# Gate projections moved among the convolution's taps, other PSUM banks for a values projection, and two products moved to the front of the Strassen stage

## The chip, the cores and the metric

The kernel runs on one core of one Trainium2 chip. The metric is the device time of one execution in microseconds. A core has five engines with an instruction queue each: TensorE (PE, matmuls; PEld are its weight loads), VectorE (DVE), ScalarE (ACT), GpSimd (POOL) and SyncE (SP, which here only issues transfers). An engine works through its queue in order and waits on semaphores of the others.

## What is computed

One layer of a trunk with four token mixers side by side, for 512 tokens of width 2048, in float32. With `h = rms_norm(x)`, one wide projection `h @ w_in` is cut into the inputs of the branches and four merge gates:

```python
A  differential attention (8 heads, two softmax maps per head, ...)
B  sliding-window (128) grouped-query attention (16 q heads / 4 kv heads) ...
C  Mamba-2 SSD (16 heads, 2 B/C groups, state 128, conv 4, chunk 128) ...
D  Conformer convolution module (GLU -> causal depthwise conv 31 -> LayerNorm
   -> swish), causal
Each branch (width 1024) is multiplied by a SiLU gate path, projected to D_MODEL,
merged as sum_i sigmoid(g_i(h)) * branch_i, then one output projection and a
residual add.
```

The change touches the SiLU gates of branches A and D, the values of branch A, the convolution of branch D, and the four merge gates, whose projections are computed by a Strassen scheme.

## The kernel before, in words

`h` is held transposed in SBUF, split into a high part `hh` and a low part `hl` (each element is their sum). Every weight piece of 512 KB is loaded by SyncE into `wr`; ScalarE casts it to `wh` (L274) and VectorE makes the rest `wl` (L275). Each product is three matmuls: `hh·wh`, `hl·wh`, `hh·wl` (L388 to L390, with `proj`; 48 matmuls of 128x512 for 128 columns of the projection). `next_piece` prepares pieces up to six ahead in the order of the list `seq`. A scheduler that keeps the data dependencies decides, from costs that it assumes, in which order each engine gets its instructions; the kernel's text only gives the first wish.

The stages on TensorE, with their times in the profiled execution:

- to 328 us: norm, scan of branch C. Its end lies beside `values(0)`, the values projection for the first four heads (L617 to L619). A block of the scan loads `se` (POOL, L555), scales, exponentiates and multiplies it (L559 to L570), and its two kinds of matmul (L576, L579) add into the bank `o`, which VectorE then reads (L583). `values(0)` adds four blocks of 128 tokens in four PSUM banks: three `acc` banks and the `o` bank.
- 328 to 502 us: for each of eight channels of 128, two projections of branch D, `DV` and `DGT`. VectorE evicts them (L641, L644, with ScalarE's sigmoid and GpSimd's product L643 between) and runs 31 taps over the padded row `pad` (L646, L648) into `y`, called `keep_yl` in the trace. GpSimd adds the channels up in `csum` (L653).
- 502 to 576 us: `values(4)` for the other four heads, on the same kind of banks; the normalization over channels that needs `csum` begins beside it (`pm`).
- 576 to 665 us: eight projections `DG`, each with `silu_of` (L402 to L404: product by VectorE, sigmoid by ScalarE, product by VectorE), and the output of branch D.
- 665 to 1021 us: eight heads of differential attention, each with the projections `AQ`, `AK`, `AG` (`AG` with `silu_of`) and four blocks: scores, a biased maximum (L781), exp (L785), normalization (L786 to L789), transposes (L792), product with the values (L796).
- 1021 to 1261 us: windowed heads, in the same manner (L741 and L742 scores, L851 to L865 softmax, L869 transposes, L876 product with the values).
- 1261 to 1906 us: merge gates, eight blocks `gi` of 336 matmuls. For the first block the sums and differences of quarters of `h` are made by `make_sums` (L902 to L913: `e` pairs, written as high and low parts `s1`, `s2`, `s4` and in place of the second quarter of `hh`, `hl`), two of 16 row groups per call. A step `s1` of the list brings weights for one of eight `k`, with sums of weights made on VectorE (L235 to L237); a step `s2` those for the three products added afterwards.
- to the end: up-projections of the branches, merge, output projection.

The four accumulators of a gate block are `ba` (two `acc` banks), `bc` (`s` banks), `bd` (`tr` banks) and `bb` (`acc`, `o`). The pool `mge` behind `ev_pair()` gives `e` tiles, three buffers in turn.

Of the kernel before, what the change touches and what calls it, by code (L numbers as in the profile page):

```python
# [11 lines left out]
F32 = mybir.dt.float32  # L12
# [31 lines left out]
def build_sequence():  # L44
    seq = []

    def proj(col):
        for half in range(2):
            seq.append(("p", col, half))

    def values(h):
        for k2 in range(KT // 2):
            seq.append(("v", AV + h * P, k2 * 2, 2, S))

    for half in range(2):
        for col in (CB, CC):
            seq.append(("p", col, half))
    for g in range(2):
        if g > 0:
            proj(CB + g * P)  # L60
            proj(CC + g * P)
        for j in range(4):
            proj(CX + (g * 4 + j) * P)
        for j in range(4):
            proj(CZ + (g * 4 + j) * P)
    values(0)
    for c in range(NB):
        proj(DV + c * P)
        proj(DGT + c * P)
    values(4)  # L70
    for c in range(NB):
        proj(DG + c * P)
    for h in range(8):
        proj(AQ + h * P)
        proj(AK + h * P)
        proj(AG + h * P)
    for j in range(2):
        proj(BK + j * P)
        proj(BV + j * P)
    for j in range(8):  # L80
        proj(BQ + j * P)
        proj(BG + j * P)
    for gi in range(NGATE):
        for k in range(KH):
            seq.append(("s1", gi, k))
        for r in range(3):
            for kp in range(KH // 2):
                seq.append(("s2", gi, r, kp))
# [14 lines left out]
def hybrid_trunk(ctx, tc, x, norm_w, w_in, diff_lambda, diff_subln_w, swa_sinks, ssd_conv_w,  # L103
# [50 lines left out]
    def keep(tag):  # L154
        return yp.tile([P, S], F32, tag=tag, name="keep_" + tag)
# [62 lines left out]
        return hi, lo  # L218

    def strassen_piece(key):  # L220
        gi = key[1]
        n1, n2 = columns(gi)
        sh = [P, 2, S]
        if key[0] == "s1":
# [25 lines left out]
    def make_piece(i):  # L250
        key = seq[i]
        late = False
        if key[0] in ("s1", "s2"):
            pieces[i] = strassen_piece(key)
            return
        if key[0] == "p":
# [346 lines left out]
            G.dma_start(y_d[2, g * 4 + j], y)  # L603


    banks4 = [acc_tile, acc_tile, acc_tile, o_tile]
    vtoks = []

    def values(h):
# [12 lines left out]
        for t in range(NT):  # L622
            for e in range(4):
# [9 lines left out]
    cv = []  # L633
    csum = ph.tile([P, S], F32, tag="csum", name="csum")
    for c in range(NB):
# [10 lines left out]
        V.tensor_scalar(y, pad[:, 0:S], cols[:, NV + c:NV + c + 1], col("fb", c), op0=ALU.mult, op1=ALU.add)  # L646
        for j in range(1, 31):
            V.scalar_tensor_tensor(y, pad[:, j:j + S], cols[:, NV + j * 8 + c:NV + j * 8 + c + 1], y,  # L648
                                   op0=ALU.mult, op1=ALU.add)
        if c == 0:  # L650
            G.tensor_copy(csum, y)
        else:
            G.tensor_tensor(csum, csum, y, op=ALU.add)  # L653
        cv.append(y)
    pm = s_tile(0)
    T.matmul(pm, lhsT=ones, rhs=csum, start=True, stop=True)
    mean = tmp()
# [14 lines left out]
    rd = row_of_tokens(rs)  # L672
    rbs = ph.tile([P, S], F32, tag="rbs", name="rbs")
    A.copy(rbs, rd)
    values(4)
# [86 lines left out]
    for h in range(8):  # L762
# [169 lines left out]
    def ev_pair():  # L932
        return mge.tile([P, 2, S], F32, tag="e", name="e")

    def strassen(gi, finish, extra=None):
        ba = [acc_tile(), acc_tile()]
        bc = [s_tile(0), s_tile(1)]
        bd = [tr_tile(), tr_tile()]
        bb = [acc_tile(), o_tile()]
        for k in range(KH):  # L940
            if extra is not None and k % 2 == 0:
                extra(k // 2)
            (xh, xl), (yh, yl) = next_piece(("s1", gi, k))
            ends = (k == 0, k == KH - 1)
            for bank, st, w in ((ba, lambda t: block(k, t, 0), (xh[:, 0], xl[:, 0])),
                                (bc, lambda t: stat(2, k, t), (yh[:, 0], yl[:, 0])),
                                (bd, lambda t: block(k, t, 1), (yh[:, 1], yl[:, 1])),
                                (bb, lambda t: stat(1, k, t), (xh[:, 1], xl[:, 1]))):
                for t in range(2):
                    mm3(bank[t], st(t), w, *ends)  # L950
        u2, u3 = ev_pair(), ev_pair()
        for t in range(2):
            A.copy(u2[:, t], ba[t])
# [6 lines left out]
        for r, bank in ((0, ba), (1, bd), (2, bb)):  # L960
            for kp in range(KH // 2):
                wh, wl = next_piece(("s2", gi, r, kp))
                for j in range(2):
# [11 lines left out]
                finish(r % 2, t, r // 2, bank[t] if r == 0 else u[:, t], u[:, t])  # L975

    for gi in range(NGATE):
        def finish(half, t, right, src, dst):
            tt = half * 2 + t
            n = gi % 2 * S + right * 2 * S  # L980
            A.activation(dst, src, AF.Sigmoid, scale=rst[:, tt:tt + 1])  # L981
            G.dma_start(gate_d[gi // 2, tt][:, n:n + S], dst)  # L982

        strassen(gi, finish, make_sums if gi == 0 else None)
    close_pool("mge", "mgt", "mgw", "sab", "hp")


# [181 lines left out]
```

## Time and profile before

| | before |
|---|---|
| median of 3 runs | 2449.65 us (2446.09 to 2450.25) |
| profiled execution | 2448.79 us |
| its span, first to last instruction | 2446.4 us |
| TensorE busy | 2382.8 us, 97% |
| VectorE busy | 1557.2 us, 64% |
| ScalarE busy | 944.9 us, 39% |
| GpSimd busy | 299.8 us, 12% |

The profiled execution's own time is its span and 2.4 us around it. A busy TensorE may run at either level of its clock; the profile gives the granted clock as a share of full speed.

### The profile page before, as it was taken

The page shows a single profiled execution, that of the slowest core. Times are in us where ns is not written, and L with a number is a line of the kernel's source. Part 1 is how long each engine was busy: PE and PEld are TensorE (multiplying, and loading weights), DVE is VectorE, ACT ScalarE, POOL GpSimd, SP SyncE. Part 2 cuts the span into 40 slices and gives each one's busy share as a digit, 9 for nine tenths or more (in the row PEclk, how much of TensorE's full clock was granted, in tenths as well). Part 3 has the DMA queues.
Part 4 walks back from the last instruction along what each step waited for, and adds up shares of the span by engine and source line. Part 5 has one row for each costly group of instructions (what it writes and reads, how often), then busy time and mean ns, then how long its engine had stood idle before and what let it go on. Part 6 is the DMA issues. An engine that isn't in the chain of part 4 may idle for free.

```text
span 2446.4 us, 29178 instructions
## 1 busy us (share of the span) xinstructions
PE 2382.8 (97%) x11189; PEld 1959.1 (80%) x11189; DVE 1557.2 (64%) x2496; ACT 944.9 (39%) x1439; POOL 299.8 (12%) x312
## 2 busy tenths in 40 slices
PE   8999899989999999999978999999999999999998
PEld 7877688868888888887756888888888888888888
DVE  6586449999756565465669777787777543444323
ACT  5343122212545455455544444444444322222222
POOL 0022011210311111100000000000000002322101
PEclk9999999999999999999989999999999999999999
DMA  6343243324433333333323555455556744443423
GB/s 178 86 122 104 69 112 95 95 61 112 127 106 91 92 99 87 104 91 95 95 74 112 166 166 166 150 171 163 171 167 194 258 169 146 151 146 111 156 96 112
DMA packets 292586, 309.80 MB, mean 127 GB/s; under 512 B 13198, under 2 KB 197899, under 8 KB 292446
## 3 DMA queue, kind: packets, MB, share of 16 engines
q1 hardware_dynamic: 278174, 266.71, 36.5%
q0 software_dynamic: 10784, 34.92, 4.3%
q10 hardware_dynamic: 3488, 6.30, 0.8%
q8 instruction: 87, 1.43, 0.2%
q14 instruction: 53, 0.43, 0.1%
HBM read 278.44 MB, written 29.45 MB: 126 GB/s over the span
## 4 chain that ended last, share of the span: by engine, by line
PE 87%; DVE 10%; issue 1%; DMA 1%; ACT 1%; POOL 0%; POOLq 0%; DVEq 0%; ACTq 0%
PE acc L390 10%; PE acc L388 10%; PE acc L389 10%; DVE keep_yl L648 5%; PE acc L930 3%; PE acc L929 3%; PE acc L928 3%; PE tr L929 2%; PE tr L930 2%; PE tr L928 2%; PE s L928 2%; PE s L930 2%; PE s L929 2%; PE acc L968 2%; PE acc L969 2%; PE acc L967 2%
## 5 line engine op out<-in xcount | busy, mean ns | idle before, releaser
L274 ACT CAST wh<-wr 128x1024 fp32r<-128x1024 f32 x284 | 297.6, 1050 | 782.2 <-PE acc L389 295.3
L275 DVE TENSOR_TENSOR wl<-wr,wh 128x1024 fp32r<-128x1024 f32 x284 | 363.1, 1282 | 344.6 <-ACT wh L274 341.7
L388 PE MATMUL acc<-hh,wh 128*128 128x512 f32 x1376 | 544.7, 396 | 0.1
L390 PE MATMUL acc<-hh,wl 128*128 128x512 f32 x1376 | 541.3, 394 | 0.2 <-DVE wl L275 0.2
L389 PE MATMUL acc<-hl,wh 128*128 128x512 f32 x1376 | 540.7, 393 | 0.0
L390 PEld LDWEIGHTS acc<-hh,wl 128*128 128x128 f32 x1376 | 258.8, 188 | 53.6 <-issue 1.3
L389 PEld LDWEIGHTS acc<-hl,wh 128*128 128x128 f32 x1376 | 259.1, 188 | 53.0 <-issue 1.7
L388 PEld LDWEIGHTS acc<-hh,wh 128*128 128x128 f32 x1376 | 258.8, 188 | 52.8 <-issue 2.1
L211 ACT CAST wh<-wr 128x1024 fp32r<-128x1024 f32 x128 | 133.8, 1052 | 140.6 <-PE o L930 60.0
L648 DVE SCALAR_TENSOR_TENSOR keep_yl<-pad,cols,keep_yl 128x512 f32<-128x512 f32 x240 | 176.1, 786 | 0.7
L212 DVE TENSOR_TENSOR wl<-wr,wh 128x1024 fp32r<-128x1024 f32 x128 | 155.5, 1220 | 30.7 <-ACT wh L211 30.7
L982 POOL DMA_DIRECT2D gate_d<-e x64 | 34.5, 540 | 614.0 <-ACT e L981 598.5
L1043 POOL TENSOR_TENSOR m<-m,u 128x512 f32<-128x512 f32 x48 | 73.6, 1568 | 273.4 <-DVE u L1042 273.4
L215 ACT CAST wh<-t 128x512 fp32r<-128x512 f32 x64 | 39.7, 621 | 108.7 <-PE tr L930 69.5
L929 PE MATMUL acc<-wl,yh 128*128 128x512 f32 x192 | 74.8, 390 | 0.0
L930 PE MATMUL acc<-wh,yl 128*128 128x512 f32 x192 | 74.8, 390 | 0.0
L928 PE MATMUL acc<-wh,yh 128*128 128x512 f32 x192 | 74.1, 389 | 0.0
L247 DVE TENSOR_TENSOR t<-wr,t 128x1024 f32<-128x1024 f32 x32 | 39.1, 1223 | 46.1 <-DMA wr<-in_w_in_dram 46.1
L212 DVE TENSOR_TENSOR wl<-t,wh 128x1024 fp32r<-128x1024 f32 x32 | 39.2, 1225 | 36.4 <-ACT wh L211 36.4
L402 DVE TENSOR_TENSOR keep_yl<-acc,rb 128x512 f32<-128x512 f32 x24 | 16.6, 691 | 68.0 <-PE acc L390 68.0
L235 DVE TENSOR_TENSOR vr<-vr,wr 128x512 f32<-128x512 f32 x64 | 43.8, 688 | 25.0 <-DMA wr<-in_w_in_dram 24.9
L785 ACT ACTIVATE pr<-pr,mx 128x128 f32<-128x128 f32 (+3 forms) x64 | 35.5, 556 | 58.4 <-DVE mx L783 58.3
(461 smaller groups left out, 4960.8 us busy)
## 6 DMA issues: line engine op xcount, KB each, us to landing
wr<-in_w_in_dram SPq DMA_DIRECT2D x320, 512.0 KB, 3.8
wr<-in_w_branch_dram SPq DMA_DIRECT2D x64, 512.0 KB, 3.6
vr<-in_w_in_dram SPq DMA_DIRECT2D x32, 512.0 KB, 4.5
gate_d<-e POOLq DMA_DIRECT2D x64, 256.0 KB, 3.3
gt<-gate_d SPq DMA_DIRECT2D x16, 1024.0 KB, 5.0
wr<-in_w_out_dram SPq DMA_DIRECT2D x32, 512.0 KB, 3.5
yraw<-y_d SPq DMA_DIRECT2D x8, 1024.0 KB, 7.8
y_d<-t POOLq DMA_DIRECT2D x24, 256.0 KB, 2.6
```

Of the source, the lines that this page charges most:

```text
L211: A.copy(hi, srcs[0])
L212: V.tensor_tensor(lo, srcs[0], hi.bitcast(F32), op=ALU.subtract)
L274: A.copy(hi, raw)
L275: V.tensor_tensor(lo, raw, hi.bitcast(F32), op=ALU.subtract)
L388: T.matmul(acc, lhsT=wh[:, k, :], rhs=xh, start=(n == 0), stop=False)
L389: T.matmul(acc, lhsT=wh[:, k, :], rhs=xl, start=False, stop=False)
L390: T.matmul(acc, lhsT=wl[:, k, :], rhs=xh, start=False, stop=(n == last))
L648: V.scalar_tensor_tensor(y, pad[:, j:j + S], cols[:, NV + j * 8 + c:NV + j * 8 + c + 1], y, op0=ALU.mult, op1=ALU.add)
L928: T.matmul(acc, lhsT=x[0], rhs=w[0], start=first, stop=False)
L929: T.matmul(acc, lhsT=x[0], rhs=w[1], start=False, stop=False)
L930: T.matmul(acc, lhsT=x[1], rhs=w[0], start=False, stop=last)
L1043: G.tensor_tensor(merged[t, nb], merged[t, nb], u, op=ALU.add)
```

## The change

Three edits, and an order of instructions that the scheduler makes anew for the whole kernel.

1. The 16 projections for the gates of branches D and A (`DG`, `AG`) move into the convolution's loop, two for each channel. Their SiLU results are stored in DRAM (`silu_d`) by GpSimd's queue and loaded again, by the same queue, where `silu_of` was. The taps of a channel are no longer issued in one go: they go to a list and are issued in portions between the projections of the next channel. Convolution results, `csum` and what follows are as before.
2. `values(0)` uses two `acc` banks and the two `s` banks; `values(4)` keeps three `acc` banks and `o`.
3. In the first gate block, the two products that need no sum (first quarter of `h` with the upper and lower weights) are computed first, by `first_products` with a new kind of step `s0` (L992 of the changed kernel); `make_sums` for all four parts comes between the two, and the first product is copied out (`u2`, L999) before the second adds to its bank. The steps `s1` of this block cast only the half of the weights that is still needed. The number of matmuls stays 336; the weight pieces loaded for this block go from 20 to 28.

```diff
     for c in range(NB):
         proj(DV + c * P)
         proj(DGT + c * P)
+        proj(DG + c * P)
+        proj(AG + c * P)
     values(4)
...
+    for r in range(2):
+        for kp in range(KH // 2):
+            seq.append(("s0", r, kp))
     for gi in range(NGATE):
         for k in range(KH):
             seq.append(("s1", gi, k))
-        for r in range(3):
+        for r in range(3 if gi else 2):
...
-            return halves_of(sh, x), halves_of(sh, t2[:, j], y[:, j], tag="v")
-        _, _, r, kp = key
+            if gi == 0:
+                hi, lo = halves_of([P, S], x[:, 1])
...
+        if key[0] == "s0":
+            x = wp.tile(sh, F32, tag="wr", name="wr")
+            nc.sync.dma_start(x, w_in_v[:, r * KH + 2 * kp:r * KH + 2 * kp + 2, n1:n1 + S])
+            return halves_of(sh, x)
...
-    values(0)
+    values(0, [acc_tile, acc_tile, lambda: s_tile(0), lambda: s_tile(1)])
...
+    def stored_silu(i, c, w):
+        sg = hold()
+        silu_of(proj(w + c * P), sg)
+        G.dma_start(silu_d[i, c], sg)
+
     for c in range(NB):
         vacc = proj(DV + c * P)
+        run_taps(8)
         gacc = proj(DGT + c * P)
...
         V.tensor_tensor(pad[:, 30:], vacc, sg, op=ALU.mult)
+        run_taps(31)
         y = keep("yl")
...
+        taps += conv_taps(c, pad, y)
         cv.append(y)
+        stored_silu(0, c, DG)
+        run_taps(8)
+        stored_silu(1, c, AG)
+        run_taps(8)
+    run_taps(31)
...
         sg = hold()
-        silu_of(proj(DG + c * P), sg)
+        G.dma_start(sg, silu_d[0, c])
...
         sg = keep("yl")
-        silu_of(proj(AG + h * P), sg)
+        G.dma_start(sg, silu_d[1, h])
...
+    def first_products(ba):
+
+        for r in range(2):
+            for kp in range(KH // 2):
+                wh, wl = next_piece(("s0", r, kp))
...
+                            T.matmul(ba[t], lhsT=a, rhs=b[:, j], start=(r == 0 and k == 0 and a is x[0] and b is wh),
+                                     stop=(k == KH - 1 and a is x[1]), skip_group_check=True)
+            if r == 0:
+                for kp in range(KH // 2):
+                    make_sums(kp)
+                u2 = ev_pair()
+                for t in range(2):
+                    A.copy(u2[:, t], ba[t])
+            else:
+                u = ev_pair()
+                for t in range(2):
+                    gate(0, 0, t, 0, ba[t], u[:, t])
+        return u2
```

On TensorE, the end of the scan beside `values(0)` before, where one block of the scan (alternating L576 and L579) ends and the next begins: one matmul of the projection stands between.

```order
L576 MATMUL o<-se,xdt 64x128
L579 MATMUL o<-se,prev_a 64x128
L619 MATMUL acc<-wh,hl 128x512
L576 MATMUL o<-se,xdt 64x128
L579 MATMUL o<-se,prev_a 64x128
```

The same place after (scan L593 and L596, projection L633 to L635, `s_2333` one of its two new banks): the projection goes on around the next block's first matmul, on all of its four banks, none of which is `o`.

```order
L593 MATMUL o<-se,xdt 64x128
L634 MATMUL s_2333<-wl,hh 128x512
L635 MATMUL s_2333<-wh,hl 128x512
L633 MATMUL acc<-wh,hh 128x512
L634 MATMUL acc<-wl,hh 128x512
L635 MATMUL acc<-wh,hl 128x512
L596 MATMUL o<-se,prev_a 64x128
L593 MATMUL o<-se,xdt 64x128
```

On VectorE, the end of the convolution before: the last L644, which frees an `acc` bank, stands behind 22 taps of the channel before it.

```order
L641 TENSOR_TENSOR ev<-acc,rb 128x512
L648 SCALAR_TENSOR_TENSOR keep_yl<-pad,cols,keep_yl 128x512
L275 TENSOR_TENSOR wl<-wr,wh 128x1024
L644 TENSOR_TENSOR pad<-acc,ev 128x512
L648 SCALAR_TENSOR_TENSOR keep_yl<-pad,cols,keep_yl 128x512 x2
L646 TENSOR_SCALAR keep_yl<-pad,cols 128x512
L648 SCALAR_TENSOR_TENSOR keep_yl<-pad,cols,keep_yl 128x512 x22
L644 TENSOR_TENSOR pad<-acc,ev 128x512
```

VectorE in the middle of the convolution after (L683 and L686 stand for L641 and L644, L664 for the taps, L292 for the lows, L419 and L421 are the two products of a gate's SiLU): between two lows there are at most five taps, and the taps of a channel run beside the gate projections.

```order
L683 TENSOR_TENSOR ev<-acc,rb 128x512
L292 TENSOR_TENSOR wl<-wr,wh 128x1024
L686 TENSOR_TENSOR pad<-acc,ev 128x512
L662 TENSOR_SCALAR keep_yl<-pad,cols 128x512
L664 SCALAR_TENSOR_TENSOR keep_yl<-pad,cols,keep_yl 128x512 x3
L292 TENSOR_TENSOR wl<-wr,wh 128x1024
L664 SCALAR_TENSOR_TENSOR keep_yl<-pad,cols,keep_yl 128x512 x4
L419 TENSOR_TENSOR hd<-acc,rb 128x512
L664 SCALAR_TENSOR_TENSOR keep_yl<-pad,cols,keep_yl 128x512
L292 TENSOR_TENSOR wl<-wr,wh 128x1024
L664 SCALAR_TENSOR_TENSOR keep_yl<-pad,cols,keep_yl 128x512
L421 TENSOR_TENSOR hd<-hd,ev 128x512
```

On TensorE at the start of the Strassen stage after (L917 is the product with the values of the last windowed head; L969 to L971 are the products of the steps `s1`, here into the `tr` banks `bd`): the first half of the first products stands ahead of these rows, and behind the head's last product come the products with the changed quarter of `hh` and `hl`. Before, L928 into `acc`, which needs no sum, stood in this place.

```order
L910 MATMUL tr<-ident,pb 128x128 x4
L917 MATMUL o<-pT,keep_yh 64x128 x4
L969 MATMUL tr<-wh,hh 128x512
L970 MATMUL tr<-wl,hh 128x512
L969 MATMUL tr<-wh,hh 128x512
L970 MATMUL tr<-wl,hh 128x512
L971 MATMUL tr<-wh,hl 128x512 x2
```

On ScalarE at the same place after, with the numbers of the buffers (L948 are the casts of `make_sums`, L999 the copy of the first product): the copy into `e_10247` stands behind the third call's casts and ahead of the fourth's, and of the three `e` buffers it gets the one that `e_10216` had.

```order
L948 CAST s1h_10076<-e_10216 128x512
L948 CAST hh_101<-e_10215 128x2x256
L948 CAST s2h_10078<-e_10215 128x512
L948 CAST s4h_10080<-e_10216 128x512
L999 COPY e_10247<-acc_10082 128x512
L999 COPY e_10247<-acc_10083 128x512
L948 CAST s1h_10076<-e_10232 128x512
```

## Rows read from the trace of the kernel before

**Rows 1.** The page: busy time of each engine; TensorE's granted clock in 40 slices.

```profile
PE 2382.8 (97%) x11189; PEld 1959.1 (80%) x11189; DVE 1557.2 (64%) x2496; ACT 944.9 (39%) x1439; POOL 299.8 (12%) x312
...
PEclk9999999999999999999989999999999999999999
```

**Rows 2.** Waits of TensorE: line, what it waited for, total us, times, longest.

```profile
PE acc L617 <- DVE pad L644: 10.9, 1, 10.9
PE acc L928 <- ACT s1h L907: 8.4, 2, 4.3
PE acc L929 <- DVE wl L212: 5.5, 2, 5.3
PE o L576 <- DVE se L567: 5.3, 1, 5.3
...
PE acc L928 <- ACT wh L211: 3.7, 1, 3.7
```

**Rows 3.** Stretches: length, busy us and count by engine, clock, DMA share, GB/s.

```profile
core 0: us, PE busy (x) PEld busy (x) DVE busy (x) ACT busy (x) POOL busy (x), PEclk, DMA share, GB/s
273.00:325.00 52.00, 39.59 (x244) 32.05 (x243) 24.82 (x52) 13.20 (x15) 12.29 (x11) 0.87 0.21 62
...
355.00:500.00 145.00, 145.00 (x642) 120.08 (x641) 133.91 (x174) 33.47 (x35) 18.59 (x12) 1.00 0.35 95
500.00:545.00 45.00, 33.32 (x140) 26.53 (x139) 45.00 (x62) 5.11 (x6) 8.31 (x6) 0.91 0.20 59
...
850.00:890.00 40.00, 40.00 (x201) 33.58 (x200) 24.24 (x54) 20.13 (x43) 5.19 (x5) 1.00 0.34 94
...
1247.00:1261.30 14.30, 10.62 (x66) 7.03 (x65) 8.66 (x47) 8.02 (x26) 0.54 (x1) 0.76 0.27 92
1261.30:1366.00 104.70, 86.89 (x338) 67.76 (x337) 92.35 (x123) 48.82 (x66) 3.78 (x7) 0.89 0.39 119
```

**Rows 4.** Timeline, TensorE after a wait: start us, duration, line, operation.

```profile
1272.09 0.63 PE L930 MATMUL acc<-wh,hl 128*128 128x512 f32 x1
...
1272.52 0.63 PE L929 MATMUL acc<-wl,hh 128*128 128x512 f32 x1
```

**Rows 5.** Timeline of GpSimd at the scan's end.

```profile
291.49 2.43 POOL L570 TENSOR_TENSOR se<-se,hd 128x1024 f32<-128x1024 f32 x1 [8.76 <-ACT se L569]
293.87 0.58 POOL L555 DMA_DIRECT2D se<-acum_d  x1
```

**Rows 6.** Timeline of VectorE: taps beside L643, and taps undisturbed.

```profile
434.29 2.45 DVE L648 SCALAR_TENSOR_TENSOR keep_yl<-pad,cols,keep_yl 128x512 f32<-128x512 f32 x2
...
528.56 13.33 DVE L648 SCALAR_TENSOR_TENSOR keep_yl<-pad,cols,keep_yl 128x512 f32<-128x512 f32 x20
```

**Rows 7.** Groups by line, 355 to 500 us: count, busy us, mean ns, idle before.

```profile
L648 DVE SCALAR_TENSOR_TENSOR keep_yl<-pad,cols,keep_yl 128x512 f32<-128x512 f32 x129 | 96.3, 793 | 0.5
L275 DVE TENSOR_TENSOR wl<-wr,wh 128x1024 fp32r<-128x1024 f32 x26 | 31.6, 1215 | 8.6 <-ACT wh L274 8.6
...
L643 POOL TENSOR_TENSOR ev<-ev,rb 128x512 f32<-128x512 f32 x6 | 12.8, 2142 | 101.9 <-ACT ev L642 101.9
L653 POOL TENSOR_TENSOR csum<-csum,keep_yl 128x512 f32<-128x512 f32 x2 | 4.5, 2240 | 20.4 <-DVE keep_yl L648 20.4
```

**Rows 8.** One line, L810, once a head: count, durations, first and last start.

```profile
L810 DVE SCALAR_TENSOR_TENSOR t<-tr,slw,keep_yl x8: 744/744/752, 745.6 to 1021.3; 128x512 f32<-128x512 f32 x8
```

**Rows 9.** Groups of VectorE by line, 1261.3 to 1366 us.

```profile
L902 DVE TENSOR_TENSOR e<-hh,hl 128x1024 f32<-128x1024 f32 x8 | 9.6, 1219 | 0.0
...
L910 DVE TENSOR_TENSOR e<-e 128x512 f32<-128x512 f32 x4 | 2.7, 685 | 0.0
```

**Rows 10.** Groups by line in one head, 850 to 889.4 us.

```profile
L402 DVE TENSOR_TENSOR keep_yl<-acc,rb 128x512 f32<-128x512 f32 x1 | 0.7, 692 | 2.3 <-PE acc L390 2.3
...
L794 ACT COPY aT<-tr 128x512 f32<-128x512 f32 x1 | 0.6, 574 | 0.0
```

**Rows 11.** The page's DMA issues: count, KB each, us to landing.

```profile
gate_d<-e POOLq DMA_DIRECT2D x64, 256.0 KB, 3.3
```

More of the change, by code (lines that the diff above doesn't have):

```diff
@@ L75, in build_sequence @@
         proj(AK + h * P)
-        proj(AG + h * P)
     for j in range(2):
@@ L603, in hybrid_trunk, with values @@
             G.dma_start(y_d[2, g * 4 + j], y)
-    banks4 = [acc_tile, acc_tile, acc_tile, o_tile]
     vtoks = []
-    def values(h):
+    def values(h, banks4):
         accs = [bank() for bank in banks4]
@@ L628, in values, with run_taps, conv_taps, tap @@
                     V.tensor_scalar(vd, vs, rst[:, t:t + 1], None, op0=ALU.mult)
-    values(0)
+    values(0, [acc_tile, acc_tile, lambda: s_tile(0), lambda: s_tile(1)])
     ph = next_phase("conv")
     cv = []
+    silu_d = dram.tile([2, NB, P, S], F32, name="silu_d")
     csum = ph.tile([P, S], F32, tag="csum", name="csum")
+    taps = []
+    def run_taps(n):
+        for _ in range(min(n, len(taps))):
+            taps.pop(0)()
+    def conv_taps(c, pad, y):
+        def tap(j):
+            w = cols[:, NV + j * 8 + c:NV + j * 8 + c + 1]
+            if j == 0:
+                V.tensor_scalar(y, pad[:, 0:S], w, col("fb", c), op0=ALU.mult, op1=ALU.add)
+            else:
+                V.scalar_tensor_tensor(y, pad[:, j:j + S], w, y, op0=ALU.mult, op1=ALU.add)
+            if j == 30 and c == 0:
+                G.tensor_copy(csum, y)
+            elif j == 30:
+                G.tensor_tensor(csum, csum, y, op=ALU.add)
+        return [lambda j=j: tap(j) for j in range(31)]
+    def stored_silu(i, c, w):
+        sg = hold()
+        silu_of(proj(w + c * P), sg)
+        G.dma_start(silu_d[i, c], sg)
     for c in range(NB):
         vacc = proj(DV + c * P)
+        run_taps(8)
         gacc = proj(DGT + c * P)
@@ L644, in hybrid_trunk @@
         V.tensor_tensor(pad[:, 30:], vacc, sg, op=ALU.mult)
+        run_taps(31)
         y = keep("yl")
[L646 to L653, printed above, removed]
-        cv.append(y)
+        taps += conv_taps(c, pad, y)
+        cv.append(y)
+        stored_silu(0, c, DG)
[3 more added lines that the diff above has]
+    run_taps(31)
     pm = s_tile(0)
@@ L674, in hybrid_trunk @@
     A.copy(rbs, rd)
-    values(4)
+    values(4, [acc_tile, acc_tile, acc_tile, o_tile])
     for c in range(NB):
         sg = hold()
-        silu_of(proj(DG + c * P), sg)
+        G.dma_start(sg, silu_d[0, c])
         u = ph.tile([P, S], F32, tag="u", bufs=4, name="u")
@@ L933, in ev_pair, with gate, strassen @@
         return mge.tile([P, 2, S], F32, tag="e", name="e")
-    def strassen(gi, finish, extra=None):
+    def gate(gi, half, t, right, src, dst):
+        tt = half * 2 + t
+        n = gi % 2 * S + right * 2 * S
+        A.activation(dst, src, AF.Sigmoid, scale=rst[:, tt:tt + 1])
+        G.dma_start(gate_d[gi // 2, tt][:, n:n + S], dst)
+    def first_products(ba):
+        for r in range(2):
+            for kp in range(KH // 2):
+                wh, wl = next_piece(("s0", r, kp))
+                for j in range(2):
+                    k = 2 * kp + j
+                    for t in range(2):
+                        x = block(r * KH + k, t, 0)
+                        for a, b in ((x[0], wh), (x[0], wl), (x[1], wh)):
+                            T.matmul(ba[t], lhsT=a, rhs=b[:, j], start=(r == 0 and k == 0 and a is x[0] and b is wh),
[6 more added lines that the diff above has]
+                    A.copy(u2[:, t], ba[t])
+            else:
+                u = ev_pair()
+                for t in range(2):
+                    gate(0, 0, t, 0, ba[t], u[:, t])
+        return u2
+    def strassen(gi, finish):
         ba = [acc_tile(), acc_tile()]
@@ L939, in strassen @@
         bb = [acc_tile(), o_tile()]
+        u2 = first_products(ba) if gi == 0 else None
         for k in range(KH):
-            if extra is not None and k % 2 == 0:
-                extra(k // 2)
             (xh, xl), (yh, yl) = next_piece(("s1", gi, k))
             ends = (k == 0, k == KH - 1)
-            for bank, st, w in ((ba, lambda t: block(k, t, 0), (xh[:, 0], xl[:, 0])),
+            for bank, st, w in ((ba, lambda t: block(k, t, 0), (xh[0], xl[0])),
                                 (bc, lambda t: stat(2, k, t), (yh[:, 0], yl[:, 0])),
                                 (bd, lambda t: block(k, t, 1), (yh[:, 1], yl[:, 1])),
[L948 to L951, printed above, removed]
+                                (bb, lambda t: stat(1, k, t), (xh[1], xl[1]))):
+                if w[0] is not None:
+                    for t in range(2):
+                        mm3(bank[t], st(t), w, *ends)
+        if gi > 0:
+            u2 = ev_pair()
+            for t in range(2):
+                A.copy(u2[:, t], ba[t])
+        u3 = ev_pair()
         for t in range(2):
-            A.copy(u2[:, t], ba[t])
             V.tensor_tensor(u2[:, t], u2[:, t], bc[t], op=ALU.add)
@@ L959, in strassen @@
             finish(1, t, 1, u3[:, t], u3[:, t])
-        for r, bank in ((0, ba), (1, bd), (2, bb)):
+        for r, bank in ((0, ba), (1, bd), (2, bb))[0 if gi else 1:]:
             for kp in range(KH // 2):
@@ L977, in hybrid_trunk @@
     for gi in range(NGATE):
[L978 to L984, printed above, removed]
+        strassen(gi, lambda *a: gate(gi, *a))
     close_pool("mge", "mgt", "mgw", "sab", "hp")
```

18 lines of the change are left out of this document (13 added, 5 removed).

## The prediction, made before the changed kernel was run

> **What bounds the kernel.** I read the page first: TensorE is busy 97% of the span, at a granted clock of nearly full height [rows 1]. The other engines matter only where they hold TensorE up, so the next view is the list of TensorE's waits [rows 2]. It has three spots: the values projection beside the end of the scan (L576), the second values projection at the end of the convolution (L617, 10.9 us in one piece), and the start of the Strassen gates (L928, L929). The table of stretches [rows 3] shows what each costs. A matmul of 128x512 takes 145.00 / 642 = 0.226 us where TensorE never stops (355 to 500 us; I use 0.227 below), and 0.43 us at the low one of the two clock levels [rows 4]; after a long wait about ten matmuls run at that pace. So a wait of 5 us costs some 7. By matmul counts and these two prices, 273 to 325 us loses 52.00 − 39.59 = 12.4 us idle and some 4 in slow matmuls: **16.7**. 500 to 545 us loses 45.00 − 33.32 = 11.7 with what follows it: **13.8** (10.9 of wait, 2.9 slow). 1261.3 to 1366 us loses 104.70 − 86.89 = 17.8 idle and about 10 slow matmuls after each wait.
>
> The number of matmuls is the same before and after, so the change can only win back these losses or make new ones. The sum is made against the profiled execution, 2448.79 us (span 2446.4), which lies 0.9 under the median of the runs, 2449.65.
>
> **A. Values projection on other banks.** Before, the fourth bank is the scan's own output bank, so its share of the projection must wait for the last scan block, and while a block waits for its decay chain (5.3 us before L576 the longest [rows 2]) nothing of that fourth bank can fill in. What makes blocks late is the chain: load of `se` on GpSimd's queue, scale, exp, product, GpSimd product. The load for the fourth block was issued at 293.87 us, right behind the 2.43 us product L570 [rows 5], and its matmuls came at 302.41: 8.5 us later. After, all four banks are free from the start, and TensorE's order has 25, 28 and 24 projection matmuls (5.7, 6.4, 5.4 us) between the blocks where before everything of the first three banks was used up. From block to block that makes 5.4 to 6.4 us of projection and 3 of scan products, against 8.5 to 10 us of chain, and two chains are in flight at once: 0 to 2 us of waiting stay. Gain between 12 (the clock does not recover) and 16.7 (all); I take **15**.
>
> **B. Gate projections among the taps.** Before, a channel has two projections on TensorE (96 × 0.227 = 21.8 us) and VectorE has 31 taps, 4 lows and 3 more: it is busy 133.91 of 145 us and falls behind; its rest, 22 taps in one row before the last L644, is what L617 waits for. After, a channel is four projections, 192 × 0.227 = 43.6 us. VectorE has 31 taps of 0.67 (20 in 13.3 us when nothing disturbs them [rows 6]) to 0.79 (mean [rows 7]), 8 lows of 1.14 to 1.22, six operations of 0.69 and some 2 us of wait for GpSimd's product: 20.8 to 24.5, plus 9.1 to 9.8, plus 4.1, plus 2 = 36 to 40.4 of 43.6 us. So TensorE stays the bound there. At the end 14 taps and 3 lows stand behind the last projection, 14 × 0.79 + 3 × 1.2 = 14.7 us, and then the sum on GpSimd, 2.2 [rows 7]: 17 us. The matmul on that sum stands 99 matmuls = 22.5 us into values(4), so it is hidden; if that cover were gone, it would cost 17. The last L686, which frees values(4)'s bank, now has two whole projections behind it. I take **13** of the 13.8; bound 8, if the later reductions of the normalization (rows that stand 169 and 194 matmuls in) come late.
>
> **C. Attention heads without their gate projection.** A head takes (1021.3 − 745.6) / 7 = 39.4 us [rows 8] and TensorE is busy without a gap. After it is 39.4 − 48 × 0.227 = 28.5 us. VectorE's part per head is 24.2 us [rows 3]; the gate takes away two operations of 0.69 [rows 10] and two lows of 1.14: 20.5 us are left, in 28.5. With the waits inside the softmax chain, which VectorE sits through (I count 3.5 us a head), it is 24, or 85%. By the matmuls between them in TensorE's order, at 0.227 us each, the scores of a block now stand 13 to 20 us ahead of its transposes, before 8 to 12; only the first head has 7. I take a loss of **2**; bounds 0 and 10.
>
> **D. Start of the Strassen stage.** Before, the last window head's tail leaves TensorE 10.62 us busy of 14.30 [rows 3], then waits of 3.7, 5.3 and twice 4.2 us follow [rows 2]. After, 48 of the first products (10.9 us) fill the tail of the last window head. But the tail then ends later: its softmax chain starts behind them. Before, from the last projection at 1247 to the end of the head it was the whole stretch of 14.30 us [rows 3]; after, the 48 products and the scores between them take 13 us (to 1259.8), and the last block's exp, normalization, transposes and product with the values come behind: more than 4 us, since four engines follow one another, less than that stretch of 14.3, which holds four blocks; I take 9. The head ends near 1268.6 instead of 1261.3. Next in TensorE's order stand 12 products with the changed low half (`hl`) and 12 with `s2`. For these VectorE works through 3 operations of 128x1024 at 1.14 and 16 of 128x512 at 0.60 (the durations of [rows 9] without the 0.08 by which neighbours overlap): 13 us, to 1281.7. Then 24 matmuls, the first ones slow: 1289.6. The other 48 first products add to the same bank, so they come behind its copy (L999), and ScalarE has that copy behind the casts of the third step of the sums, because `e_10247` takes the buffer of `e_10216`, as the order shows. VectorE's part until that buffer is free is 17 us more (1298.8), two copies of 0.6 [rows 10] follow: 1300.1. TensorE waits again for some 10 us. From there nothing is late: 60 matmuls to 1316, then 204 × 0.227 = 46.3, with the lows made faster than used (3.6 us of VectorE for 4.1 of TensorE). With a microsecond for small waits the gate block ends near 1363.5, before at 1366. I take **+2**; bounds −4 (the tail at its long end) and +8.
>
> The Trainium skill says of this order, under "TensorE: Matmul & The Clock Gate" (Part 2, step by step), that only weight loads are pulled ahead of running matmuls and that matmuls stay in program order. By it the 48 ready products cannot step past the copy's wait; were they free to, D would gain 10 us more.
>
> **E. Traffic.** 16 stores and 16 loads of 256 KB on GpSimd's queue and 8 pieces of 512 KB more on SyncE's: GpSimd is busy 12% [rows 1], the gate loads are issued a head before their use, the DMA engines are busy 0.34 of the time in the heads [rows 3]. I count nothing; if one of them were not hidden, it would cost its 3.3 us [rows 11].
>
> **Sum.** 2448.8 − 15 − 13 + 2 − 2 = 2420.8; beside the median of the runs 2421.5.
>
> **Rivals.** (1) *VectorE becomes the bound in the heads, in part*: for it speaks that its chain now has 28.5 us instead of 39.4, and that each block's scores wait for banks and `pr` buffers; against it the 4 us to spare. 1 to 3 us a head, 8 to 24 in all: 2430 to 2445. (2) *The first products are covered better*, the copy is not late, or the head's tail is short: 10 more, 2411. (3) *The convolution becomes VectorE's*: a tap beside a GpSimd operation takes 1.22 us instead of 0.67 (two in 2.45 us [rows 6]), and there are stores on GpSimd now. By rows each GpSimd product costs two or three taps 0.55 us more, 1.1 to 1.7 us, twice in a channel: inside the range above. If all taps took 1.0 us, a channel would be 31 + 9.5 + 6 = 46.5, 3 us over: 8 × 3 = 24, giving 2445. The Trainium skill, "SBUF — State Buffer", section "Who interferes with whom", has it that a VectorE instruction with two SBUF inputs and a GpSimd instruction that reads SBUF lock each other out whole. By it each of the 16 GpSimd products would stop VectorE for at most its whole 2.1 to 2.2 us [rows 7], an estimate of 35 us over the stage or 4.4 a channel, which would use up the spare 3 to 7 us and come out near this rival's time; that the taps beside L643 take longer, and not that they stop, is what the row shows. (4) *The other side, slower*: a head's softmax chain, not its matmuls, sets its length. It decides from 32.9 us a head on: the gain without C is 30, so it needs (30 + 5) / 8 = 4.4 us over 28.5. VectorE, with 20.5 us of work, would have to lose 12 us a head to waiting where I count 3.5. At 34 us a head: 2448.8 − 30 + 44 = 2463. (5) *The change does nothing*, because waits move along whole, as the Strassen start nearly does: 2449.
>
> **How the numbers follow.** Forecast 0.60; (1) 0.15; (2) 0.11; (3) 0.05; (4) 0.04; (5) 0.05. Predicted 2421.5. Low end: all of A and B, nothing in C, and (2): 2448.8 − 16.7 − 13.8 − 11 = 2407; high end: 12 + 8 − 10 − 4 = 6, so 2443. Eight in ten lie between 2410 and 2437, with half of (1). A difference of 0.2% (5 us) is about what can be told from no change; faster are forecast, (2), most of (1) and (3): 0.90; within 0.2%: 0.05; slower: 0.05.
>
> **What would show it.** Right: no wait of L633 to L635 over 2 us near 300 us; TensorE without a gap from 328 us to the end of values(4), some 90 us later than before; heads 28.5 us apart; a wait of about 13 us at L969 and one of about 10 at L992 in the Strassen start. Wrong: heads 30 us or more apart with TensorE waiting for VectorE; waits on `pad` or on a low in the convolution; no wait for L999.

## The result, and the profile after

The changed kernel takes 2421.03 us (median of 4 runs, 2419.61 to 2422.88) beside 2448.03 of the kernel before in the same set; the ratio is 0.989, with a 95% interval of 0.9873 to 0.9907. It is faster by 27 us. 2421.5 was predicted. The sum was right; terms of it were not, and their errors cancelled.

The page after: busy time of each engine, and TensorE's granted clock in 40 slices (for [rows 1]).

```profile
PE 2370.2 (98%) x11189; PEld 1953.0 (81%) x11189; DVE 1561.9 (65%) x2500; ACT 929.5 (38%) x1429; POOL 314.0 (13%) x344
...
PEclk9999999999999999999979999999999999999999
```

The number of matmuls is the same, 11189. VectorE has as much to do as before. The slice of low clock in the middle, the Strassen start, went from 8 tenths to 7.

TensorE's waits after (for [rows 2]), the longest ones behind the kernel's first 200 us.

```profile
PE tr L969 <- ACT hh L948: 12.2, 1, 12.2
PE acc L992 <- ACT e L999: 11.6, 1, 11.6
...
PE tr L1041 <- DVE e L1030: 2.7, 1, 2.7
PE o L917 <- ACT pT L913: 2.2, 3, 1.2
```

Of the list before, the wait on `pad` and those beside the scan are gone whole. In place of the four waits of 17.6 us at the Strassen start stand two, of 12.2 and 11.6 us, at the two places that the prediction named (13 and 10), and one of 2.7 that it did not.

Stretches after, with the columns of [rows 3]: the scan's end, the convolution, the heads, the last windowed head behind its last projection, and the start of the Strassen stage.

```profile
core 0: us, PE busy (x) PEld busy (x) DVE busy (x) ACT busy (x) POOL busy (x), PEclk, DMA share, GB/s
273.50:325.00 51.50, 51.50 (x312) 41.89 (x311) 26.55 (x55) 16.22 (x18) 11.80 (x11) 1.00 0.31 92
355.00:690.00 335.00, 335.00 (x1479) 277.50 (x1478) 279.24 (x353) 78.49 (x85) 33.45 (x41) 1.00 0.40 114
850.00:900.00 50.00, 50.00 (x259) 42.64 (x258) 37.90 (x94) 27.53 (x70) 12.24 (x9) 1.00 0.33 91
1214.20:1237.70 23.50, 20.13 (x123) 15.58 (x122) 15.49 (x52) 14.69 (x32) 0.55 (x1) 0.92 0.52 168
1237.70:1312.50 74.80, 50.41 (x196) 38.66 (x192) 64.98 (x95) 30.38 (x48) 1.62 (x3) 0.80 0.33 105
```

The reader is to see three things. At the scan's end TensorE has no idle time and 312 matmuls in 51.5 us, where before it had 244 in 52. From the convolution to the heads TensorE is full and VectorE is not: 279.24 of 335 us are 83%, inside the 36 to 40.4 of 43.6 that the prediction gave it. In the last two rows TensorE has 23.50 − 20.13 + 74.80 − 50.41 = 27.8 us of idle time, where the rows of before (1247 to 1261.3 and on to 1366) had 21.5; those run to the end of the first gate block, and the rows after end within it. The whole stretch, from the same start to the same end, stands under term D below.

One line in each head, as in [rows 8]:

```profile
L851 DVE SCALAR_TENSOR_TENSOR t<-tr,slw,keep_yl x8: 746/751/752, 817.4 to 1009.8; 128x512 f32<-128x512 f32 x8
```

(1009.8 − 817.4) / 7 = 27.5 us from head to head, 28.5 predicted; TensorE has no idle time in the stretch of heads shown above (50.00 of 50.00 us).

### The profile page after: what moved, and what is told of

Read it like the earlier page. It is cut to its first block, busy times and chain, and to the rows that moved or that the text cites. A ratio compares the mean times of both kernels' runs of the same rounds, so it can differ in the third digit from the quotient of the medians.

```text
span 2419.8 us, 29275 instructions
## 1 busy us (share of the span) xinstructions
PE 2370.2 (98%) x11189; PEld 1953.0 (81%) x11189; DVE 1561.9 (65%) x2500; ACT 929.5 (38%) x1429; POOL 314.0 (13%) x344
## 5 line engine op out<-in xcount | busy, mean ns | idle before, releaser
L291 ACT CAST wh<-wr 128x1024 fp32r<-128x1024 f32 x284 | 298.2, 1052 | 814.4 <-PE acc L406 304.6
L292 DVE TENSOR_TENSOR wl<-wr,wh 128x1024 fp32r<-128x1024 f32 x284 | 360.4, 1271 | 341.6 <-ACT wh L291 338.2
L213 ACT CAST wh<-wr 128x1024 fp32r<-128x1024 f32 (+1 forms) x136 | 138.9, 1026 | 146.3 <-PE o L971 59.0
L214 DVE TENSOR_TENSOR wl<-wr,wh 128x1024 fp32r<-128x1024 f32 (+1 forms) x136 | 161.2, 1190 | 39.3 <-ACT wh L213 39.1
L664 DVE SCALAR_TENSOR_TENSOR keep_yl<-pad,cols,keep_yl 128x512 f32<-128x512 f32 x240 | 180.0, 750 | 5.7
L1111 POOL TENSOR_TENSOR m<-m,u 128x512 f32<-128x512 f32 x48 | 73.6, 1569 | 273.7 <-DVE u L1110 273.7
L971 PE MATMUL acc<-wh,yl 128*128 128x512 f32 x192 | 74.8, 389 | 0.0
L969 PE MATMUL acc<-wh,yh 128*128 128x512 f32 x192 | 74.1, 389 | 0.0
L969 PE MATMUL tr<-wh,hh 128*128 128x512 f32 x128 | 48.4, 403 | 12.8 <-ACT hh L948 12.2
L214 DVE TENSOR_TENSOR wl<-t,wh 128x1024 fp32r<-128x1024 f32 x28 | 34.3, 1225 | 30.4 <-ACT wh L213 30.4
L970 PE MATMUL tr<-wl,hh 128*128 128x512 f32 x128 | 51.4, 402 | 0.0
```

The lines of the kernel that those rows point to most:

```text
L213: A.copy(hi, srcs[0])
L214: V.tensor_tensor(lo, srcs[0], hi.bitcast(F32), op=ALU.subtract)
L291: A.copy(hi, raw)
L292: V.tensor_tensor(lo, raw, hi.bitcast(F32), op=ALU.subtract)
L664: V.scalar_tensor_tensor(y, pad[:, j:j + S], w, y, op0=ALU.mult, op1=ALU.add)
L969: T.matmul(acc, lhsT=x[0], rhs=w[0], start=first, stop=False)
```

## Experiments

The runs were made in three sets; medians of the kernel before in them were 2448.65, 2449.63 and 2447.59 us, and each ratio is to those of its own set.

**The parts alone.** Four kernels, each made of the changed kernel's own lines, and E8, which tells the two halves of the banks' edit apart.

E1 is the kernel before with this edit alone:

```diff
-    values(0)
+    values(0, [acc_tile, acc_tile, lambda: s_tile(0), lambda: s_tile(1)])
```

> The kernel before with values(0) on two acc and the two s banks and nothing else. If the end of the scan is repaired by the banks alone, as term A has it, the 14.8 us that the changed kernel's trace shows less idle and slow time between 275 and 325 us come back here alone: about 2433 us, with no wait over 1 us at the projection's lines beside the scan. Rival: the repair comes from the new order as a whole (the store and load traffic and the gates moved GpSimd's and VectorE's queues too); then this kernel gains clearly less than 12 us, 2440 or more.

Measured: 2430.55 us, 0.9931 (0.9919 to 0.9944), 18 us less. The stretch at the scan's end in E1:

```profile
273.00:325.00 52.00, 52.00 (x313) 42.26 (x312) 25.98 (x56) 16.52 (x23) 11.81 (x11) 1.00 0.33 101
```

This is the row of the changed kernel, by the banks alone, with GpSimd's and VectorE's old traffic. The rival falls.

E8 keeps the third `acc` bank and gives up only the scan's:

```diff
-    values(0)
+    values(0, [acc_tile, acc_tile, acc_tile, lambda: s_tile(0)])
```

> The kernel before with values(0) on three acc banks and one s bank: only the scan's bank o is given up, the third acc bank is kept. If the shared o bank is the cause (term A), the same as e1, 2430.5 within 2 us. If the third acc bank held things up too, part of the 18 us is missing: 2435 or more.

Measured: 2432.27 us, 0.9932 (0.9919 to 0.9946). The same as E1 (17 us less): it is the shared bank `o`, not the number of `acc` banks.

E2 has the first edit alone, the gate projections in the convolution's loop.

```diff
         proj(DGT + c * P)
+        proj(DG + c * P)
+        proj(AG + c * P)
...
-    for c in range(NB):
-        proj(DG + c * P)
```

> The kernel before with the gate projections moved among the taps and nothing else (old banks, old Strassen start). Theory, term B and C: the 10.9 us wait on pad and its slow matmuls go, the heads shrink to 28.5 us without a wait: 14 us less, about 2434 us, and the waits at the scan's end and at the Strassen start stand as before. Rival (heads bound by VectorE): 2440 or more, with TensorE waiting in the heads.

Measured: 2430.54 us, 0.9929 (0.9916 to 0.9941), 18 us less; the wait on `pad` is gone, and those of the two other places stand as before:

```profile
PE acc L951 <- ACT s1h L930: 8.1, 2, 4.2
PE acc L952 <- DVE wl L211: 5.9, 2, 5.3
...
PE o L575 <- DVE se L566: 5.3, 1, 5.3
PE acc L951 <- ACT wh L210: 3.7, 1, 3.7
```

E3 has the Strassen start alone.

```diff
+    for r in range(2):
+        for kp in range(KH // 2):
+            seq.append(("s0", r, kp))
...
+        u2 = first_products(ba) if gi == 0 else None
```

> The kernel before with the first products and the new order of the sums and nothing else. By the changed kernel's trace (two waits of 12 us each for 17.8 idle before) this part loses 2 to 4 us: about 2451 us. By the prediction's term D it gains 2: 2446. If it gains 5 or more, the loss in the changed kernel comes from the two other parts moving the heads' end, not from this part.

Measured: 2453.65 us, 1.0019 (1.001 to 1.0028), 5 us more. With nothing else changed, the two waits of the changed kernel are there:

```profile
PE tr L946 <- ACT hh L925: 12.2, 1, 12.2
PE acc L635 <- DVE pad L662: 10.9, 1, 10.9
PE acc L969 <- ACT e L976: 10.7, 1, 10.7
```

E4 is the changed kernel with the old Strassen start.

```diff
-    for r in range(2):
-        for kp in range(KH // 2):
-            seq.append(("s0", r, kp))
```

> The changed kernel with the old Strassen start (banks and gates alone). If the three parts add up: 2448 less 15 less 14, 2419, that is 2 to 3 us under the changed kernel. If the first products help after all (term D as predicted), 2423 or more.

Measured: 2417.02 us, 0.9873 (0.986 to 0.9887): 4 us under the changed kernel by the medians. The two intervals overlap, but E3, on the other side, resolves the same loss. Two of the three edits make the whole gain, and the third costs 4 to 5 us of it. E4 has the lowest median of the kernels that compute the whole layer here.

The parts alone do not simply add up. E1 and E2 gain 18 us each, 36 together; E4, which has both edits, gains 31.6, and with the other edit in place each of them is worth 2430.55 − 2417.02 = 13.5 us. The intervals leave that open. In the profiled executions some of it lies ahead of both edits: the first matmul of `values(0)` starts at 271.5 us in E1 and at 271.2 in E2, in the kernel before at 273.5, and in E4, the changed kernel and E8 at 273.1, 273.7 and 274.9.

**Why the convolution no longer stops TensorE.** E7 is E4 with the gate of branch A back in the heads, so that a channel has three projections.

```diff
         proj(DGT + c * P)
         proj(DG + c * P)
-        proj(AG + c * P)
...
-        stored_silu(1, c, AG)
-        run_taps(8)
```

> The changed kernel with the old Strassen start and with only the gate of branch D among the taps; the gate of branch A stays in the heads. A channel is three projections, 32.7 us of TensorE, against 33 to 37 us of VectorE by the prediction's prices. If it is the ratio of VectorE's to TensorE's work per channel that made the 10.9 us wait on pad (term B), part of it comes back: waits of 3 to 10 us on pad or a low, 2420 to 2428. If one projection behind the last L686 is cover enough, none comes back and the time is that of e4, 2417. The heads go back to 39.4 us; by term C that costs nothing either way.

Measured: 2418.58 us, 0.9875 (0.9861 to 0.9888), no difference from E4, and no wait on `pad`. The convolution's stretch in E7; the last product into `pad`, with its start; and the first matmul of `values(4)`:

```profile
355.00:580.00 225.00, 225.00 (x994) 186.36 (x993) 219.66 (x277) 52.48 (x56) 29.19 (x24) 1.00 0.37 105
```

```profile
583.12 0.68 DVE L668 TENSOR_TENSOR pad<-acc,ev 128x512 f32<-128x512 f32 x1
...
589.52 0.39 PE L615 MATMUL acc<-wh,hh 128*128 128x512 f32 x1
```

VectorE is busy 219.66 of 225 us, 98%, more than before the change (133.91 of 145 [rows 3]), and TensorE still doesn't wait. So the part of my term B that says TensorE is safe because VectorE has time to spare in a channel is not what is needed. With taps in portions and one projection (48 × 0.227 = 10.9 us) behind the last channel's two, the bank that the last product into `pad` gives back is free 5.7 us before the first matmul of `values(4)`; the taps left over are not what that waits for. Whether the portions alone, with no projection moved, would be enough was not tried. The same run speaks to term C: a kernel whose heads have their gate and one whose heads have not take the same time.

**What bounds the Strassen start.** E5 takes away the copy that the second products wait for. They go to the banks `bb`, are added to the first by VectorE, and the copy moves to the end of the block.

```diff
-                            T.matmul(ba[t], lhsT=a, rhs=b[:, j], start=(r == 0 and k == 0 and a is x[0] and b is wh),
+                            T.matmul((ba, bb)[r][t], lhsT=a, rhs=b[:, j], start=(k == 0 and a is x[0] and b is wh),
...
                 u = ev_pair()
                 for t in range(2):
-                    gate(0, 0, t, 0, ba[t], u[:, t])
+                    A.copy(u[:, t], ba[t])
+                for t in range(2):
+                    V.tensor_tensor(u[:, t], u[:, t], bb[t], op=ALU.add)
+                    gate(0, 0, t, 0, u[:, t], u[:, t])
```

> The changed kernel, with the second of the two first products in the two banks bb instead of on top of the first, added to it by VectorE afterwards; so no copy stands between them, and the first product is copied at the end as in the other gate blocks. The sums still come between the two in the text. The order has 18 of the second 48 matmuls ahead of the head's end and 30 behind it. If the copy's late buffer is what TensorE waits for at L992, the 11.6 us wait goes, and the 12.2 us at L969 shrinks by 30 x 0.227 = 6.8: about 2405 us. Rival: VectorE, which makes the sums without a gap from 1238 to 1274, is the bound of this stretch whatever stands between; then the waits come back as waits for later sums and the gain is under 6 us: 2415 or more.

Measured: 2421.11 us, 0.9884 (0.9871 to 0.9898). No difference from the changed kernel, where 2405 was expected; the rival came. The copy's wait is gone, and its time is not won: it comes back in waits for the sums, of which the longest, on `hh`, add up to 15.4 us. (The edit gives VectorE two more operations of 128x512.)

E6 has E5's edit, and all sums behind both products:

```diff
             if r == 0:
-                for kp in range(KH // 2):
-                    make_sums(kp)
...
+                for kp in range(KH // 2):
+                    make_sums(kp)
```

> As e5, with all sums behind both products in the text. The order on TensorE is the same up to the first sum's product; behind it each step's four products stand together, where e5 has the products without bb first. If only the cover by 96 matmuls without sums counts, the same as e5 within 3 us, about 2405. If VectorE's rate of sums bounds the steps (about 7 us of VectorE for two steps of 8.2 us of TensorE), the two differ by the waits in the first steps, and e6 is the slower one.

Measured: 2421.17 us, 0.9886 (0.9872 to 0.9899). TensorE's costliest wait in E6, and the stretch behind its last windowed head:

```profile
PE acc L969 <- ACT s1h L948: 19.4, 4, 8.3
```

```profile
1215.00:1238.50 23.50, 22.15 (x132) 17.36 (x132) 15.22 (x52) 14.08 (x32) 0.55 (x1) 1.00 0.52 168
1238.50:1312.00 73.50, 49.94 (x169) 36.65 (x166) 68.88 (x99) 32.33 (x51) 1.63 (x3) 0.79 0.36 118
```

VectorE is busy 68.88 of 73.50 us, TensorE 49.94. The same two stretches of E4, with the old start:

```profile
1214.30:1229.20 14.90, 11.24 (x67) 7.68 (x65) 8.65 (x47) 8.03 (x26) 0.54 (x1) 0.67 0.25 89
1229.20:1299.00 69.80, 50.98 (x184) 38.31 (x182) 69.31 (x96) 31.06 (x45) 0.54 (x1) 0.83 0.32 102
```

Here VectorE has 0.5 us of idle time in 69.8 us. Behind the head, VectorE does some 69 us of work in either stretch. What differs is when this work can begin: 14.9 us after the last projection in E4, 23.5 in E6, because TensorE sets 48 or more products between the scores of the last head.

E12 spreads the sums over the steps, as before the change, behind all 96 products:

```diff
         for k in range(KH):
+            if gi == 0 and k % 2 == 0:
+                make_sums(k // 2)
             (xh, xl), (yh, yl) = next_piece(("s1", gi, k))
```

> e6 with the four parts of the sums spread over the steps as in the kernel before (a part ahead of each two steps), behind 96 matmuls that need no sum. If only the lump of 36 us of sums without a weight's low between them made e5 and e6 as slow as the changed kernel, this one gains on both and on e4: 2405 to 2412. If VectorE's whole work is what counts, it stays at 2417 to 2421.

Measured: 2420.67 us, 0.9887 (0.9873 to 0.9902): the order of the sums in the text changes nothing.

E9 and E10 take work from VectorE. The sums leave out the low parts of `h`: the eight additions of 128x1024 are not made. E9 is the changed kernel, E10 is E4, with this edit:

```diff
-        for x, o in ((x1, 0), (x2, 2)):
-            V.tensor_tensor(x, hhq[q + o][:, r:r + 2].bitcast(F32), hlq[q + o][:, r:r + 2].bitcast(F32), op=ALU.add)
+        h1, h2 = hhq[q][:, r:r + 2].bitcast(F32), hhq[q + 2][:, r:r + 2].bitcast(F32)
```

> The changed kernel, which leaves out of the sums the low parts of h: the 8 additions hi plus lo (L943, 9.1 us of VectorE) are not made, the sums are built from the high parts alone; matmuls, loads and casts are as before. If VectorE's work, in its order, sets the length of the first gate block, 6 to 9 us go: about 2413. Rival: the loads of the weights through three wr buffers (28 pieces now, 5.4 us of VectorE waiting for a load) or the order on TensorE set it; then no more than 3 us go: 2418 or more.

Measured: 2411.22 us, 0.9847 (0.9833 to 0.9862), 10 us less than the changed kernel. Its two waits both shrink, by 9.2 us together:

```profile
PE acc L991 <- ACT e L998: 7.5, 1, 7.5
PE tr L968 <- ACT hh L947: 7.1, 1, 7.1
```

> e4 (old Strassen start) with the same 8 additions left out. Here VectorE is busy 69.31 of 69.80 us behind the last windowed head, so by VectorE's work 7 to 9 us go: 2409. If the gain here is the same as in e9, the two starts are bound by the same thing; if TensorE's order is the bound, 2414 or more.

Measured: 2402.77 us, 0.9814 (0.9799 to 0.9828), 14 us less than E4, more than the 9.1 that were taken away. The stretch as in E4, from the head's end:

```profile
1229.20:1299.00 69.80, 60.74 (x248) 46.47 (x245) 67.77 (x97) 36.62 (x53) 1.62 (x3) 0.95 0.40 129
```

TensorE now has 248 matmuls in the 69.8 us where it had 184, and 64 × 0.227 us are 14.5. Its idle time fell from 69.80 − 50.98 = 18.8 us to 69.80 − 60.74 = 9.1, by 9.8; the other 4.8 are matmuls that no longer run at the low level, and the mean granted clock is 0.95 instead of 0.83. In E9 the two long waits stay, only shorter, and the slow matmuls behind each of them stay too.

E11 is E4 with the eight additions on GpSimd, which is idle here; it leaves nothing out.

```diff
-            V.tensor_tensor(x, hhq[q + o][:, r:r + 2].bitcast(F32), hlq[q + o][:, r:r + 2].bitcast(F32), op=ALU.add)
+            G.tensor_tensor(x, hhq[q + o][:, r:r + 2].bitcast(F32), hlq[q + o][:, r:r + 2].bitcast(F32), op=ALU.add)
```

> e4 with the 8 additions on GpSimd, which is idle there. Nothing is left out. It takes 9.1 us from VectorE; but an addition of 128x1024 took GpSimd 2.43 us (L570), and by the taps beside L643 VectorE gets 1.22 us operations instead of 0.67 meanwhile, so 8 additions of 2.4 us take back some 8 us. Theory: a gain of 0 to 4, 2413 to 2417. If GpSimd and VectorE do not hinder each other here: as e10, 2409.

Measured: 2421.21 us, 0.9891 (0.9875 to 0.9908), 4 us more than E4; I had expected 0 to 4 less. The additions on GpSimd in E11 (count, busy us, mean ns), and the timelines of VectorE and of GpSimd where the first three of them run:

```profile
L925 POOL TENSOR_TENSOR e<-hh,hl 128x1024 f32<-128x1024 f32 x8 | 24.4, 3063 | 39.9 <-DVE s2l L931 37.4 <-DVE s4l L931 2.4
```

```profile
1230.16 1.28 DVE L234 TENSOR_TENSOR vr<-vr,wr 128x512 f32<-128x512 f32 x2
1231.36 5.60 DVE L235 TENSOR_TENSOR wr<-wr 128x512 f32<-128x512 f32 x2
1236.88 2.83 DVE L216 TENSOR_TENSOR wl<-vr,wh 128x512 fp32r<-128x512 f32 x1
1239.64 0.68 DVE L234 TENSOR_TENSOR vr<-vr,wr 128x512 f32<-128x512 f32 x1
...
1231.14 8.02 POOL L925 TENSOR_TENSOR e<-hh,hl 128x1024 f32<-128x1024 f32 x3
```

GpSimd takes 3.06 us each in the mean where L570 took 2.43 [rows 5]. In the 8 us of three additions VectorE gets three operations of 128x512 done, at 2.8 us each; the same kind of operation takes 0.68 right behind them. The Trainium skill ("SBUF — State Buffer", section "Who interferes with whom") says that a VectorE instruction with two SBUF inputs and a GpSimd instruction that reads SBUF exclude each other; these rows agree: VectorE does one operation for each addition. Over the whole span VectorE is busy 1564.8 us in E11 and 1561.1 in E4, though the eight additions (9.1 us) are no longer its own: what is left to it takes 13 us longer. So the additions on GpSimd cost VectorE more than they save it. The prediction, under rival (3), read [rows 6] as taps that take longer and do not stop; these operations last as long as the addition beside them.

## Why the prediction was right, and where it was not

That the time came out within 0.5 us of the forecast is luck: A, B and C together were to gain 26 us, and E4, which has them without D, gains 31.6; D was to gain 2 and loses 4 to 5.

**A, 15 predicted.** Right in mechanism and size: the trace of the changed kernel has no idle time there, and E1 and E8 give 18 and 17 us, with intervals of 13 to 20 that hold 15. In E1's row TensorE has 313 matmuls in the 52 us where before it had 244, and 69 × 0.227 us are 15.7, if they are all of 128x512. The bank `o` is the cause.

**B, 13 predicted, and C, a loss of 2.** E2 measures them together: 18 us (14.4 to 20.6 by its interval) where 11 were predicted; beside E1's edit they are worth 13.5 (E4). The wait on `pad` went whole, as said. C's 2 us of loss do not show: TensorE has no wait in the heads, and E4 is not slower than E7. The wait with its slow matmuls accounts for 13.8 us; what the further microseconds of E2 are is open, but for the 2.3 us of its profiled lead that lie ahead of the edit. The step of B that argued from VectorE's load in a channel reached a true end (no wait) by a condition that E7 shows is not needed. Rival (3), a convolution bound by GpSimd beside VectorE, did not come: the 240 taps that have this form keep VectorE busy 180.0 us after and 176.1 before, 0.75 and 0.73 us each:

```profile
L648 DVE SCALAR_TENSOR_TENSOR keep_yl<-pad,cols,keep_yl 128x512 f32<-128x512 f32 x240 | 176.1, 786 | 0.7
...
L664 DVE SCALAR_TENSOR_TENSOR keep_yl<-pad,cols,keep_yl 128x512 f32<-128x512 f32 x240 | 180.0, 750 | 5.7
```

**D, a gain of 2 predicted, 4 to 5 of loss measured.** This is the step that failed. Its chain was right in most places: two waits at L969 and at L992 with the named causes and nearly the named lengths, as its signs of being right had it. The stretch from the last projection of the windowed heads to the last product of the first gate block, before, after and in E4, and the part of it after that lies behind the wait at L992 (columns of [rows 3]):

```profile
1247.00:1367.00 120.00, 98.50 (x407) 75.59 (x407) 102.01 (x171) 57.84 (x93) 4.32 (x8) 0.87 0.38 116
...
1214.20:1339.70 125.50, 95.00 (x415) 74.25 (x415) 100.17 (x171) 56.77 (x94) 4.33 (x8) 0.85 0.42 134
...
1214.30:1335.30 121.00, 98.53 (x407) 75.92 (x406) 102.31 (x172) 57.85 (x93) 4.32 (x8) 0.86 0.36 117
...
1269.60:1339.70 70.10, 66.77 (x268) 52.87 (x269) 53.41 (x75) 31.75 (x45) 3.24 (x6) 0.94 0.55 173
```

By the prediction the stretch takes 1363.5 − 1247 = 116.5 us; it takes 125.5. The tail of the last head is 1.5 us of these 9: 23.5 us behind the last projection, against 22 taken (13 + 9). Most of them lie in the sentence "From there nothing is late", which was wrong: from the start of the second products the prediction has 1363.5 − 1300.1 = 63.4 us, and 70.1 were needed, with 3.3 us of idle time (the wait of 2.7 us at L1041 above all) and slow matmuls. In VectorE's timeline of the changed kernel the work after the last sums begins late; ScalarE's cast that it waits for stands last:

```profile
1273.32 0.69 DVE L949 TENSOR_TENSOR s4l<-e,s4h 128x512 fp32r<-128x512 f32 x1
1278.93 1.83 DVE L214 TENSOR_TENSOR wl<-wr,wh 128x1024 fp32r<-128x1024 f32 x2 [4.92 <-ACT wh L213]
...
1285.12 0.69 DVE L237 TENSOR_TENSOR vr<-vr,wr 128x512 f32<-128x512 f32 x1 [3.21 <-DMA wr<-in_w_in_dram]
...
1277.84 1.05 ACT L213 CAST wh<-wr 128x1024 fp32r<-128x1024 f32 x1 [4.99 <-PE acc L992]
```

After the sums VectorE waits for weights (4.9 us for a cast, 3.2 for a load): 28 pieces go through three buffers each of `wr`, `wh` and `wl`, the cast waits for a buffer that the second products hold, and these stood behind the copy. Term E, which counted nothing for the loads, has here a load that is not hidden. VectorE's work in the whole stretch did not grow (100.17 us, before 102.01); it stands idle for 25 us of it, before for 18.

Rival (2), and the sentence that D would gain 10 us more were the 48 products free of the copy, fall with E5, E6 and E12: free of it, they gain nothing. In place of the copy the runs show VectorE: it is busy 69 us of the 70 to 74 behind the last windowed head in E4 and E6, and 9.1 us less of its work give 10 (E9) and 14 us (E10). The first products give TensorE something to do in the head's tail, but they delay the end of that head by 9 us (23.5 instead of 14.3), and VectorE, which works in order, has its sums behind it; it waits for the head's last product:

```profile
1238.15 0.69 DVE L922 TENSOR_TENSOR t<-o,keep_yl 128x512 f32<-128x512 f32 x1 [3.51 <-PE o L917]
```

That this delay makes the loss of 4 to 5 us is read from the traces; a kernel whose first products do not delay the head was not tried.

**The rivals (1) and (4)** did not come: VectorE is busy 37.90 of 50 us in the heads, and TensorE does not wait.

## What to carry to other kernels

Before idle time of one engine is filled, look at the busy share of the engine that it waits for in that same stretch, not in the whole span: where that one is full, as VectorE is behind the head before the change,

```profile
1261.30:1331.00 69.70, 51.89 (x184) 38.88 (x183) 69.15 (x95) 31.08 (x45) 0.54 (x1) 0.83 0.34 102
```

(69.15 of 69.70 us), work that filled the gaps only moved the waits here. Look which bank a stage shares with the one beside it before you count banks: one other bank gave 17 us. The wait at the end of the convolution went with one projection behind the loop's last dependence and the taps in portions, while VectorE stayed 98% busy in the loop: the loop's own balance did not have to change.

## What was not expected of the hardware

Eight additions moved from VectorE to an idle GpSimd made the kernel 4 us slower: beside them VectorE's operations of 0.68 us took 2.8, one for each addition, and the additions took 3.06 us in the mean instead of the 2.43 of L570. And E10's gain is half as large again as the work that it leaves out (14 us for 9.1): 4.8 us of it are matmuls at the high level of TensorE's clock that had run at the low one (granted clock 0.95 instead of 0.83 in the stretch).
